# Three edits to a hybrid decoder layer in split FP32 on one core: the first two projection slots interleaved by k step, two weight units in other buffers, a fixed order for the last group

## Chip, core and metric

The kernel runs on one NeuronCore of one Trainium2 chip, in one launch. The metric is the device time of one execution in microseconds (us). Engines are named as in the profile: PE is TensorE, ACT is ScalarE, DVE is VectorE, POOL is GpSimd, SP is SyncE, which here only issues transfers.

## What is computed

One decoder layer on x of 512 tokens and 1024 channels, all in float32:

```python
u = rms_norm(x, norm_mix_pre)
proj = u @ w_in                    # ten slots of 256 columns, four gates of 1024
y_a, y_b, y_c, y_d = ...           # gated recurrence, pooling, HGRN2, short convolution
branch_out = einsum("btkc,kcd->btkd", ys, w_branch)
merged = sum_k sigmoid(gate_k) * branch_out_k
h = x + rms_norm(merged @ w_out, norm_mix_post)
u = rms_norm(h, norm_mlp_pre)
hid = square(relu(u @ w_up))       # 4096 wide
h = h + rms_norm(hid @ w_down, norm_mlp_post)
```

## The kernel before, in words

**Products in three passes.** Every large product is taken from operands that are split into a high and a low half. `split` (L160) lets ACT make the high half (a rounding copy) and DVE the low half (the difference). `mm3` (L240) then adds three matmuls: high by high, high by low, low by high. A matmul has 128 rows, 128 columns of weights and mostly 512 moving columns.

**Weights.** All weights but the down projection's come in units of 128x1024 (512 KB) from `wts`. `load` (L149) issues the transfers on SP into three raw buffers, `prep` (L164) splits a unit into one of six pairs `whi`, `wlo`, and `unit` (L232) hands out the next one while it prepares up to four units ahead. `Wt` holds the counters. Units 66 and 67, the last two of the output projection, are an exception (`SPARE`): they go into two tiles of the pool `up`. That pool has four tiles, which first hold `uh` and `ul`, the halves of the transposed input (L257), and later `u2h` and `u2l`, the halves of the second norm's output (L860).

**The start (L276 to L294, L358).** The input comes transposed in eight tiles of 128x512 (`xT`, `xload` L146), one for each k step of the contraction. `xsplit` (L265) scales a tile by `gmix`, a column of the parameter tile `par_s`, and makes its two halves. The first unit is cut in three (`LOADCUT`). Eight small matmuls on a tile of ones (`WARM`) run while the first transfers come. Then `slot_mm` (L336) makes one slot of 256 columns: for each of eight k steps two column halves of 128 with three matmuls each, into two PSUM banks. A slot needs two units, k steps 0 to 3 and 4 to 7. Slots follow one another: `b0`, `b1`, `b2`, then `p_x` and so on. The pool `mm` of PSUM has four banks, which `b0` and `b1` fill. `b2` lies in the pool `sm`. The fourth slot, `p_x` (L385), takes the four banks over once `evac` (L349) has multiplied the sums by `rstd_bc`. That is the token norm, which comes from `do_rstd` (L316) and is spread over the partitions by two matmuls in `bc_rstd` (L330), called in the middle of `b2`.

**The output projection (L782 to L894).** `e0` makes columns 0 to 511 of four token tiles. `out_mm` (L829) makes columns 512 to 1023 of one token tile, with units 64 to 67 in `wu`. `chain` (L843) turns the sums of a tile into h and into the input of the up projection: square and sum, root (`row_rstd`), two passes over 1024 columns. `trans` and `put` (L863, L872) transpose it and split it, `put(t, 0, ..)` for k steps 0 to 3 into `u2h[0]`, `u2l[0]`, `put(t, 1, ..)` for k steps 4 to 7 into `u2h[1]`, `u2l[1]`. The first up projection (`up_mm`, L906) starts with k steps 0 to 3 of tokens 0 to 255.

**The MLP.** `up_pair` (L968) makes 256 hidden columns, `up_out` (L919) takes relu (ACT), square (ACT) and the split. `down_group` multiplies groups of 512 hidden channels by a scheme of seven products. Only the last group (L1038 to L1070) is made plainly: four units `us`, two hidden pairs `aa[0]` and `aa[1]` (pairs 14 and 15), and for each token tile t two pieces of 512 columns, the last tile's second piece in two of 256. Each piece is added to `macc` (L1052), squared and summed (`sq_only`, `sq_tot`), multiplied by the gain (`gain`, L1029). After the root (`row_rstd`, L812) `half` (L1032) scales, adds h and sends the result out.

**What sets the order.** The kernel is written in Tile, which places the instructions of each engine by a simulated timeline, so the order of the program differs from that of the text, except for calls inside `keep_in_program_order`. On the chip each engine's queue runs strictly in the order placed, and waits on semaphores.

Of the kernel before, what the change touches and what calls it, by code (L numbers as in the profile page):

```python
# [41 lines left out]
for _n, _w in (("gmix", 8), ("convw", 8), ("convb", 2), ("ba", 2), ("bx", 2), ("lam", 2),  # L42
               ("pscale", 2), ("lb", 2), ("hnorm", 1), ("sconv", 6), ("invw", 2), ("corr", 32), ("bo", 2)):
    PAR[_n] = (_o, _w)
    _o += _w
# [4 lines left out]
def tile_hybrid_trunk(ctx: ExitStack, tc: tile.TileContext, xT, xn, wts, dn, par, bd, cst, msk, gains, out):  # L50
# [65 lines left out]

    xt = [ap_.tile([P, 2, T], F32, tag="acc", name=nm("xt")) for _ in range(4)]
# [24 lines left out]
    spare = []  # L142
    LOADCUT = {0: ((0, 256), (256, 512), (512, D))}
    xfirst = [0, 1, 2]

    def xload(k):  # L146
        nc.sync.dma_start(xt[k // 2][:, k % 2], xT[k])

    def load(n):  # L149
        while Wt.n_load < min(n, NU):  # L150
            i = Wt.n_load
            r = rp.tile([P, D], F32, tag="raw", name=nm("raw"))
            for o, e in LOADCUT.get(i, ((0, D),)):
                if i == 0 and xfirst:
                    xload(xfirst.pop(0))
                nc.sync.dma_start(r[:, o:e], wts[i, :, o:e])
            Wt.raw[i] = r
            Wt.n_load += 1
# [5 lines left out]
    def prep(n):  # L164
        while Wt.n_prep < min(n, NI):
# [15 lines left out]
            for o, e in LOADCUT.get(i, ((0, D),)):  # L181
                if i == 0 and xorder[0] == 0:
                    xorder.pop(0)
                    xsplit(0, lambda: split(hi[:, o:e], lo[:, o:e], r[:, o:e]))
                    continue
                split(hi[:, o:e], lo[:, o:e], r[:, o:e])
                if i == 0:
                    xsplit(xorder.pop(0))
# [39 lines left out]
    extra = []  # L228
    ahead = [4]
    WARM = 8  # L230

    def unit():  # L232
# [3 lines left out]
        if extra:  # L236
            extra.pop(0)()
# [25 lines left out]
    xorder = [0, 1, 2]  # L263

    def xsplit(k, between=None):  # L265
        src = xt[k // 2][:, k % 2]
        g = prm("gmix", k)
# [4 lines left out]
        if between:  # L272
            between()
# [4 lines left out]
    act.activation(wrm, ones[:, :1].bitcast(F32), AF.Sigmoid)  # L278
    nc.scalar.dma_start(par_s[:, :NPAR], par)
    load(1)  # L280
# [3 lines left out]
    xload(3)  # L284
    load(2)
    for k in range(4, NK):
        xload(k)
    load(3)
    prep(1)
    xsplit(3)  # L290
    prep(2)
    for k in range(4, NK):
        xsplit(k)
# [18 lines left out]
    extra[:] = [lambda: load_x(0), lambda: load_x(1), lambda: load_x(2), lambda: load_x(3), load_consts]  # L312
# [45 lines left out]
    b0 = slot_mm()  # L358
    b1 = slot_mm()
# [668 lines left out]

    def gain(t, a, b):  # L1029
        dve.tensor_tensor(mgs[t][:, a:b], cm(t, a, b), g2[:, a:b], ALU.mult)  # L1030

    def half(t, r, a, b):  # L1032
        m = mgs[t][:, a:b]
        dve.scalar_tensor_tensor(m, m, r, hr[t // 2][:, t % 2, a:b], ALU.mult, ALU.add)
        eng = nc.scalar if t == NT - 1 and a == T else nc.sync
        eng.dma_start(out[t * P : t * P + P, a:b], m)

    us = [unit() for _ in range(GF)]  # L1038
    aa = [[x_[:, :4].rearrange("p (c h) t -> p c (h t)", c=2) for x_ in hid.pop(NPAIR - 2 + s)] for s in range(2)]
    for t in range(NT):  # L1040
        bk = dn_bank()
        pieces = [(0, T, bk[:, 0]), (T, 2 * T, bk[:, 1])]
        if t == NT - 1:
            pieces[1:] = [(T, T + 256, bk[:, 1, :256]), (T + 256, D, up_bank()[:, 0, :256])]
        for pi, (a, b, ps) in enumerate(pieces):
# [5 lines left out]
            m = cm(t, a, b)  # L1051
            dve.tensor_tensor(m, m, ps, ALU.add)  # L1052
            sq_only(m, 4 + t, pi)
            if pi < 1 or t < NT - 1:
                v = sq_tot(4 + t, pi, stat[:, t, 6:7] if pi == 0 else v, 3 + pi)
            if pi == 0:
                mgs[t] = hp.tile([P, D], F32, tag="h", name=nm("mg"))
            if t < NT - 1 or pi < 2:
                gain(t, a, b)
        if t == NT - 1:  # L1060
            v = sq_tot(4 + t, 1, v, 4)
            v = sq_tot(4 + t, 2, v, 5)
        r = row_rstd(v, 4 + t, (lambda: gain(t, T + 256, D)) if t == NT - 1 else None)
        if t == NT - 1:
            half(t, r, 0, T)
            half(t, r, T, T + 256)
            half(t, r, T + 256, D)
        else:
            for a, b in ((0, T), (T, D)):
                half(t, r, a, b)  # L1070


def _layout(inp):
# [5 lines left out]
    xt = x.T.reshape(NK, P, T)  # L1079
    xn = x.reshape(NT, P, D)  # L1080
# [12 lines left out]
    for n in SLOT_ORDER:  # L1093
        slot(wi, SLOT[n])
    for k in GATE_ORDER:
# [23 lines left out]
    def cols(v):  # L1119
# [6 lines left out]
        a["norm_mix_pre"][0].reshape(8, P).T,  # L1126
# [26 lines left out]
    return [xt, xn, wts, dn, par, bd, cst, msk, gains]  # L1153
# [21 lines left out]
```

## Time and profile before

| | us |
|---|---|
| median of 3 runs (751.07 to 751.37) | 751.09 |
| profiled execution, its own time | 751.62 |
| its span, first to last instruction | 749.8 |
| PE busy in the span | 738.3 (98%) |
| DVE busy | 537.7 (72%) |
| ACT busy | 312.2 (42%) |

The span runs from the first to the last instruction on the core; the execution's own time is taken around it. PE's busy time includes matmuls that overlap in the pipeline: one of 512 columns takes 0.39 from its start to its end, and in a dense row the next one starts well before that end. So the starts of matmuls tell more than their busy time.

### The profile page before, as it was taken

How to read it: one execution, taken by the hardware profiler on the slowest of the kernel's cores; microseconds unless marked ns; L12 is line 12 of the kernel's file. 1: busy time of each engine (PE TensorE's matmuls, PEld its weight loads, DVE VectorE, ACT ScalarE, POOL GpSimd, SP SyncE). 2: the span in 40 equal slices, each digit the busy share in tenths (PEclk: the TensorE clock that was granted, in tenths of full speed). 3: DMA queues.
4: the chain of work that ended last, by engine and by line, in shares of the span. 5: the costliest groups of instructions: out<-in, count | busy, mean ns of one | idle time of the engine just before them, and what ended most of it. 6: DMA issues, size and time to landing. Idle time of an engine off the chain costs nothing.

```text
span 749.8 us, 8896 instructions
## 1 busy us (share of the span) xinstructions
PE 738.3 (98%) x3508; PEld 620.5 (83%) x3508; DVE 537.7 (72%) x781; ACT 312.2 (42%) x404; POOL 6.3 (1%) x11
## 2 busy tenths in 40 slices
PE   8999999999999999999999999999999999999995
PEld 7888988888888888888888988888888888888884
DVE  5798346559997576554649585787879696977967
ACT  6524223335423322242445466544445362636322
POOL 1100000000000000000000000000000000000000
PEclk9999999999999999999999999999999999999998
DMA  9733232222222253223333514142323314050202
GB/s 327 265 116 112 85 102 95 85 85 85 84 75 95 85 185 124 98 100 111 113 113 140 202 52 169 57 140 85 135 89 109 116 64 161 6 214 33 84 1 112
DMA packets 23049, 84.59 MB, mean 113 GB/s; under 512 B 2656, under 2 KB 3424, under 8 KB 21216
## 3 DMA queue, kind: packets, MB, share of 16 engines
q1 hardware_dynamic: 22720, 83.86, 31.6%
q8 instruction: 27, 0.44, 0.2%
q10 hardware_dynamic: 288, 0.17, 0.1%
q14 instruction: 14, 0.11, 0.0%
HBM read 79.83 MB, written 4.19 MB: 112 GB/s over the span
## 4 chain that ended last, share of the span: by engine, by line
PE 96%; DVE 2%; DMA 1%; issue 1%; SPq 0%; ACT 0%; DVEq 0%; ACTq 0%
PE mm L242 15%; PE mm L243 15%; PE mm L241 15%; PE ub L241 8%; PE ub L243 8%; PE ub L242 8%; PE db L243 7%; PE db L241 7%; PE db L242 7%; PE sm L571 2%; PE sm L243 1%; PE sm L242 1%; PE sm L241 1%; DMA raw<-in_wts_dram 1%; PE sm L680 0%
## 5 line engine op out<-in xcount | busy, mean ns | idle before, releaser
L161 ACT ACTIVATE whi<-raw 128x1024 fp32r<-128x1024 f32 (+2 forms) x104 | 108.7, 1045 | 250.0 <-PE mm L242 123.1
L162 DVE TENSOR_TENSOR wlo<-raw,whi 128x1024 fp32r<-128x1024 f32 (+2 forms) x104 | 124.8, 1200 | 74.0 <-ACT whi L161 73.4
L242 PE MATMUL mm<-ul,whi 128*128 128x512 f32 x384 | 149.7, 391 | 0.6 <-DVE ul L274 0.6
L243 PE MATMUL mm<-uh,wlo 128*128 128x512 f32 x384 | 149.2, 390 | 0.0
L241 PE MATMUL mm<-uh,whi 128*128 128x512 f32 x384 | 148.8, 393 | 0.4 <-ACT whi L161 0.4
L241 PE MATMUL ub<-u2h,whi 128*128 128x512 f32 (+1 forms) x288 | 105.4, 367 | 1.0 <-DVE u2l L162 1.0
L242 PE MATMUL ub<-u2l,whi 128*128 128x512 f32 (+1 forms) x288 | 105.3, 366 | 0.0
L243 PE MATMUL ub<-u2h,wlo 128*128 128x512 f32 (+1 forms) x288 | 105.2, 366 | 0.0
L242 PEld LDWEIGHTS mm<-ul,whi 128*128 128x128 f32 x384 | 72.3, 189 | 16.0 <-DVE ul L274 1.2
L241 PEld LDWEIGHTS mm<-uh,whi 128*128 128x128 f32 x384 | 72.1, 188 | 15.8 <-ACT whi L161 0.9
L243 PEld LDWEIGHTS mm<-uh,wlo 128*128 128x128 f32 x384 | 72.4, 188 | 15.0
L242 PE MATMUL db<-flo,ahi 128*128 128x512 f32 x196 | 76.3, 389 | 0.0
L241 PE MATMUL db<-fhi,ahi 128*128 128x512 f32 x196 | 76.3, 389 | 0.0
L243 PE MATMUL db<-fhi,alo 128*128 128x512 f32 x196 | 76.3, 389 | 0.0
L992 DVE TENSOR_TENSOR macc<-macc,db 128x1024 f32<-128x1024 f32 x42 | 51.1, 1216 | 23.1 <-PE db L243 22.4
L241 PEld LDWEIGHTS ub<-u2h,whi 128*128 128x128 f32 x288 | 54.2, 189 | 10.1 <-DVE u2l L162 1.4
L242 PEld LDWEIGHTS ub<-u2l,whi 128*128 128x128 f32 x288 | 54.3, 189 | 8.8
L243 PEld LDWEIGHTS ub<-u2h,wlo 128*128 128x128 f32 x288 | 54.3, 189 | 8.7
L161 ACT ACTIVATE fhi<-x 128x1024 fp32r<-128x1024 f32 x28 | 29.7, 1059 | 39.8 <-PE db L243 26.6
L242 PEld LDWEIGHTS db<-flo,ahi 128*128 128x128 f32 x196 | 36.8, 188 | 7.7
L241 PEld LDWEIGHTS db<-fhi,ahi 128*128 128x128 f32 x196 | 36.8, 188 | 7.6
L243 PEld LDWEIGHTS db<-fhi,alo 128*128 128x128 f32 x196 | 36.8, 188 | 7.6
(271 smaller groups left out, 1024.3 us busy)
## 6 DMA issues: line engine op xcount, KB each, us to landing
raw<-in_wts_dram SPq DMA_DIRECT2D x103, 512.0 KB, 3.3
ab<-in_dn_dram SPq DMA_DIRECT2D x14, 1024.0 KB, 4.8
t<-in_xn_dram SPq DMA_DIRECT2D x8, 512.0 KB, 8.0
xt<-in_xt_dram SPq DMA_DIRECT2D x8, 256.0 KB, 5.5
h1d<-t SPq DMA_DIRECT2D x4, 512.0 KB, 2.7
hr<-h1d SPq DMA_DIRECT2D x2, 1024.0 KB, 5.4
out_dram<-mg SPq DMA_DIRECT2D x7, 256.0 KB, 2.0
t<-in_gains_dram SPq DMA_DIRECT2D x2, 512.0 KB, 6.2
```

The source lines that it names most:

```text
L161: act.activation(hi, src, AF.Copy)
L162: dve.tensor_tensor(lo, src, hi.bitcast(F32), ALU.subtract)
L241: pe.matmul(ps, lh, rh, start=first, stop=False)
L242: pe.matmul(ps, lh, rl, start=False, stop=False)
L243: pe.matmul(ps, ll, rh, start=False, stop=last)
L571: pe.matmul(bk[ct][:, cs].rearrange("s (h n b) -> s h n b", h=2, b=B), kk_[:, ct, cs], qo, start=True, stop=True)
L992: dve.tensor_tensor(macc[p], macc[p], ps, ALU.add)
```

## The change

Three edits, with a smaller layout change for the first.

1. The first two slots run together. `x0` is a new input, the first x tile with the eight columns of `gmix` beside it, so `par_s` loses these. Units 1 and 2 are swapped in the layout, so that units 0 and 1 are k steps 0 to 3 of both slots and units 2 and 3 k steps 4 to 7. Each k step has twelve matmuls: both slots, both column halves, three passes. Units 0 and 1 come in three cuts, the very first piece on ACT's queue. The token tiles, two more units and the constants are loaded behind (`extra` is gone), and there are seven small matmuls instead of eight.
2. Units 66 and 67 are split into tiles of the pool `acc`, the buffers of the merged branches.
3. The last group's instructions are kept in program order on PE, DVE and ACT, with the finishing of tile t - 1 (`finish`) written behind the first piece of tile t. The last tile's scaling is done in parts of 768 and 256 columns instead of 512, 256 and 256.

The core of the diff:

```diff
-    LOADCUT = {0: ((0, 256), (256, 512), (512, D))}
...
+        if k == 0:
+            nc.sync.dma_start(x0t, x0)
+        else:
+            nc.sync.dma_start(xt[k // 2][:, k % 2], xT[k - 1])
...
             if i in SPARE:
-                if not spare:
-                    spare.extend(up.tile([P, 2, D], F32R, tag="u", name=nm("sp")) for _ in range(2))
-                hi, lo = (x_[:, i - SPARE[0]] for x_ in spare)
+                hi, lo = (ap_.tile([P, D], F32R, tag="acc", name=nm("sp")) for _ in range(2))
...
+    wload(nc.scalar, 0, 0, W)
     nc.scalar.dma_start(par_s[:, :NPAR], par)
+    xload(0)
+    wload(nc.sync, 1, 0, W)
+    xload(1)
+    wload(nc.sync, 0, W, 2 * W)
+    wload(nc.sync, 1, W, 2 * W)
+    xload(2)
...
+    CUTS = {0: (0, W), 1: (W, 2 * W), 2: (2 * W, D), 4: (0, 2 * W), 6: (2 * W, D)}
+    for k in range(NK):
+        pair = (0, 1) if k < 4 else (2, 3)
+        if k in CUTS:
+            o, e = CUTS[k]
+            act.activation(fw[pair[0]][0][:, o:e], fr[pair[0]][:, o:e], AF.Copy)
+        xhi(k)
+        if k in CUTS:
+            act.activation(fw[pair[1]][0][:, o:e], fr[pair[1]][:, o:e], AF.Copy)
+        xlo(k)
+        if k in CUTS:
+            for i in pair:
+                dve.tensor_tensor(fw[i][1][:, o:e], fr[i][:, o:e], fw[i][0][:, o:e].bitcast(F32), ALU.subtract)
+        for wi, us_, first, last in ((0, uh, True, False), (0, ul, False, False), (1, uh, False, True)):
+            for s_ in range(2):
+                for c in range(2):
+                    o_ = (k % 4) * W + c * P
+                    pe.matmul(fb[s_][c], fw[pair[s_]][wi][:, o_ : o_ + P], U(us_, k),
+                              start=first and k == 0, stop=last and k == NK - 1)
...
-    b0 = slot_mm()
-    b1 = slot_mm()
     dg = do_rstd()
...
+    def add_sq(t, pi, a, b, ps):
+        m = cm(t, a, b)
+        K(dve.tensor_tensor(m, m, ps, ALU.add))
+        K(act.activation(s_tile(b - a), m, AF.Square, accum_out=stat[:, 4 + t, pi : pi + 1]))
...
+    def finish(t, rhw, cut):
+        rt, h, w = rhw
+        r = stat[:, 4 + t, 7:8]
+        K(dve.reciprocal(r, rt))
+        K(dve.scalar_tensor_tensor(w, r, h, r, ALU.mult, ALU.mult))
+        K(dve.scalar_tensor_tensor(r, w, 1.5, r, ALU.add, ALU.mult))
+        half(t, r, 0, cut)
+        half(t, r, cut, D)
...
+        for a, b, ps in pieces:
             for j in range(GF):
                 wh, wl = us[j]
-                hh, hl = aa[j // 2]
-                mm3(ps, hh[:, j % 2, t * P : t * P + P], hl[:, j % 2, t * P : t * P + P],
-                    wh[:, a:b], wl[:, a:b], j == 0, j == GF - 1)
...
+                hh, hl = (x_[:, j % 2, t * P : t * P + P] for x_ in aa[j // 2])
+                K(pe.matmul(ps, hh, wh[:, a:b], start=j == 0, stop=False))
+                K(pe.matmul(ps, hh, wl[:, a:b], start=False, stop=False))
+                K(pe.matmul(ps, hl, wh[:, a:b], start=False, stop=j == GF - 1))
+        mgs[t] = hp.tile([P, D], F32, tag="h", name=nm("mg"))
+        for pi, (a, b, ps) in enumerate(pieces):
+            add_sq(t, pi, a, b, ps)
+            if pi == 0 and prev:
+                finish(t - 1, prev, T)
+            gain(t, a, b)
+            v = tot(t, pi)
+        prev = root(v)
+    finish(NT - 1, prev, T + 256)
```

Where the order of instructions moves, at three places. First PE in the second half of the third slot (`sm_344`, `sm_345`), up to the first matmul of the fourth, `p_x`. Before (`sm_390` is the sum of `bc_rstd`, `mm_443` the first half of `p_x`; 2 and 17 matmuls of the third slot are left out at the two gaps):

```order
L241 MATMUL sm_344<-uh_109,whi_247 128x512
L332 MATMUL sm_390<-t_335,ones 128x512
L242 MATMUL sm_344<-ul_111,whi_247 128x512
...
L242 MATMUL sm_345<-ul_111,whi_247 128x512
L333 MATMUL sm_390<-t_335,ones 128x512
L243 MATMUL sm_345<-uh_109,wlo_248 128x512
...
L243 MATMUL sm_345<-uh_109,wlo_248 128x512
L241 MATMUL mm_443<-uh_108,whi_279 128x512
```

and now (`sm_400` is that sum, `mm_453` the half of `p_x`, in the bank of `mm_153`; eight and five matmuls of the third slot are left out at the two gaps):

```order
L231 MATMUL sm_345<-uh_110,wlo_353 128x512
L359 MATMUL sm_400<-t_335,ones 128x512
L229 MATMUL sm_344<-uh_110,whi_352 128x512
...
L229 MATMUL sm_345<-uh_110,whi_352 128x512
L360 MATMUL sm_400<-t_335,ones 128x512
L230 MATMUL sm_345<-ul_112,whi_352 128x512
L231 MATMUL sm_345<-uh_110,wlo_353 128x512
...
L231 MATMUL sm_345<-uh_110,wlo_353 128x512
L229 MATMUL mm_453<-uh_109,whi_358 128x512
```

The second of the pair, L333 before and L360 now, stands 19 matmuls of the third slot ahead of `p_x` before, and eight now. The third slot's first matmul is on both sides the 97th after the small ones.

Second DVE in the chain of token tile 2 of the output projection, up to the low half that the first up projection waits for. Before (`u2l_3110` is `u2l[0]`, `u2l_3151` is `u2l[1]`):

```order
L162 TENSOR_TENSOR u2l_3110<-sm_3099,u2h_3109 128x4x128
L821 RECIPROCAL stat<-rt_3088 128x1
L822 SCALAR_TENSOR_TENSOR nt_3090<-stat,nh_3089 128x1
L823 SCALAR_TENSOR_TENSOR stat<-nt_3090,stat 128x1
L848 SCALAR_TENSOR_TENSOR t_2808<-t_2969,stat,t_2808 128x1024
L162 TENSOR_TENSOR wlo_3286<-raw_2956,whi_3285 128x1024
L850 SCALAR_TENSOR_TENSOR t_2969<-t_2808,rst_101,t_2801 128x1024
L162 TENSOR_TENSOR wlo_3506<-raw_3246,whi_3505 128x1024
L162 TENSOR_TENSOR u2l_3110<-mm_3126,u2h_3109 128x4x128
L162 TENSOR_TENSOR u2l_3151<-sm_3104,u2h_3150 128x4x128
```

and now (`u2l_3122` is `u2l[0]`, `u2l_3163` is `u2l[1]`):

```order
L162 TENSOR_TENSOR u2l_3122<-sm_3111,u2h_3121 128x4x128
L846 RECIPROCAL stat<-rt_3100 128x1
L162 TENSOR_TENSOR u2l_3163<-sm_3116,u2h_3162 128x4x128
L847 SCALAR_TENSOR_TENSOR nt_3102<-stat,nh_3101 128x1
L848 SCALAR_TENSOR_TENSOR stat<-nt_3102,stat 128x1
L873 SCALAR_TENSOR_TENSOR t_2818<-t_2981,stat,t_2818 128x1024
L162 TENSOR_TENSOR wlo_3298<-raw_2968,whi_3297 128x1024
L875 SCALAR_TENSOR_TENSOR t_2981<-t_2818,rst_101,t_2811 128x1024
L162 TENSOR_TENSOR wlo_3518<-raw_3258,whi_3517 128x1024
L162 TENSOR_TENSOR u2l_3122<-mm_3138,u2h_3121 128x4x128
L162 TENSOR_TENSOR u2l_3163<-mm_3143,u2h_3162 128x4x128
```

One low half of `u2l[1]` moves from behind the last row on `u2l[0]` to the place behind the reciprocal.

Third PE at the start of the last group, behind the last matmul of up pair 15. Before (`ahi_5313` and `alo_5314` are `aa[0]`, `ahi_5520` and `alo_5521` are `aa[1]`; `db_5534`, `ub_5679`, `db_5582` are three pieces):

```order
L241 MATMUL db_5534<-whi_5459,ahi_5313 128x512
L243 MATMUL db_5534<-whi_5459,alo_5314 128x512
L241 MATMUL ub_5679<-whi_5431,ahi_5313 128x256
L242 MATMUL ub_5679<-wlo_5432,ahi_5313 128x256
...
L242 MATMUL db_5582<-wlo_5460,ahi_5313 128x512
L243 MATMUL db_5582<-whi_5459,alo_5314 128x512
L243 MATMUL ub_5679<-whi_5459,alo_5314 128x256
L241 MATMUL db_5534<-whi_5489,ahi_5520 128x512
L242 MATMUL db_5534<-wlo_5490,ahi_5520 128x512
...
L243 MATMUL db_5534<-whi_5489,alo_5521 128x512
```

and now (`ahi_5325`, `alo_5326` are `aa[0]`; `ahi_5532`, `alo_5533` are `aa[1]`; `db_5546` is tile 0's bank):

```order
L231 MATMUL ub_5470<-u2h_3162,wlo_5424 128x512
L1103 MATMUL db_5546<-whi_5443,ahi_5325 128x512
L1104 MATMUL db_5546<-wlo_5444,ahi_5325 128x512
L1105 MATMUL db_5546<-whi_5443,alo_5326 128x512
...
L1105 MATMUL db_5546<-whi_5471,alo_5326 128x512
L1103 MATMUL db_5546<-whi_5501,ahi_5532 128x512
L1104 MATMUL db_5546<-wlo_5502,ahi_5532 128x512
L1105 MATMUL db_5546<-whi_5501,alo_5533 128x512
```

Before, 18 matmuls on `aa[0]` stand ahead of the first one on `aa[1]`, and six more ahead of the first one on its low half; now there are six, and two more.

## Rows read from the trace of the kernel before

**Rows 1.** The page, the chain of work that ended last, by engine.

```profile
PE 96%; DVE 2%; DMA 1%; issue 1%; SPq 0%; ACT 0%; DVEq 0%; ACTq 0%
```

**Rows 2.** Timeline, 0 to 9 us: start us, duration us, engine, line, operation, [idle before].

```profile
1.05 3.79 PE L283 MATMUL sm<-ones 128*128 128x128 f32 x16 [1.05 <-DVE spt L526]
...
3.79 0.49 DVE L269 TENSOR_SCALAR uh<-xt,par_s 128x512 fp32r<-128x512 f32 x1 [2.79 <-DMA par_s<-in_par_dram]
...
4.59 1.22 PE L241 MATMUL mm<-uh,whi 128*128 128x512 f32 x2
...
5.61 1.05 PE L242 MATMUL mm<-ul,whi 128*128 128x512 f32 x2
...
6.47 0.78 PE L243 MATMUL mm<-uh,wlo 128*128 128x512 f32 x2
6.58 0.72 ACT L271 ACTIVATE uh<-xt,par_s 128x512 fp32r<-128x512 f32 x1 [2.03 <-DMA xt<-in_xt_dram]
...
8.23 0.64 PE L242 MATMUL mm<-ul,whi 128*128 128x512 f32 x2
```

**Rows 3.** Two stretches: bounds, busy us of each engine, granted clock, DMA share, GB/s.

```profile
9.00:12.00 3.00, 3.00 (x15) 2.21 (x13) 1.98 (x4) 2.25 (x4) 0.00 (x0) 1.00 1.05 406
408.40:416.00 7.60, 7.58 (x64) 7.58 (x65) 6.94 (x34) 6.22 (x20) 0.00 (x0) 1.00 0.36 139
```

**Rows 4.** Timeline, third slot to the start of the fourth.

```profile
29.30 0.39 PE L241 MATMUL sm<-uh,whi 128*128 128x512 f32 x1
...
36.11 0.40 PE L333 MATMUL sm<-t,ones 128*128 128x512 f32 x1
...
36.54 0.69 DVE L334 COPY rstd_bc<-sm 128x512 f32<-128x512 f32 x1
...
37.35 1.23 DVE L162 TENSOR_TENSOR wlo<-raw,whi 128x1024 fp32r<-128x1024 f32 x1
...
38.49 2.48 DVE L350 TENSOR_TENSOR t<-mm,rstd_bc 128x512 f32<-128x512 f32 x4
...
40.65 0.39 PE L241 MATMUL mm<-uh,whi 128*128 128x512 f32 x1
```

**Rows 5.** Timeline, end of the output projection, start of the up projection.

```profile
402.38 0.15 DVE L821 RECIPROCAL stat<-rt 128x1 f32<-128x1 f32 x1
402.57 0.22 DVE L822 SCALAR_TENSOR_TENSOR nt<-stat,nh 128x1 f32<-128x1 f32 x1
...
407.07 0.39 PE L243 MATMUL sm<-sp,ylo 128*128 128x512 f32 x1
...
407.68 0.69 DVE L162 TENSOR_TENSOR u2l<-mm,u2h 128x512 fp32r<-128x512 f32 x1
...
408.42 0.39 PE L241 MATMUL ub<-u2h,whi 128*128 128x256 f32 x1 [0.96 <-DVE u2l L162]
```

**Rows 6.** Timeline, start of the last group.

```profile
718.91 0.39 PE L241 MATMUL db<-whi,ahi 128*128 128x512 f32 x1
...
719.11 1.03 ACT L921 ACTIVATE q<-ub 128x1024 f32<-128x1024 f32 x1 [7.32 <-PE ub L243]
...
722.35 1.23 DVE L162 TENSOR_TENSOR alo<-q,ahi 128x1024 fp32r<-128x1024 f32 x1 [3.37 <-ACT ahi L161]
...
722.37 0.50 PE L241 MATMUL db<-whi,ahi 128*128 128x512 f32 x1
...
723.64 0.49 PE L243 MATMUL db<-whi,alo 128*128 128x512 f32 x1
```

**Rows 7.** Timeline of the end; then DVE's groups from 720 to 747 us.

```profile
740.98 0.28 PE L243 MATMUL db<-whi,alo 128*128 128x256 f32 x1
...
745.16 1.54 DVE L1034 SCALAR_TENSOR_TENSOR mg<-mg,stat,hr 128x512 f32<-128x512 f32 x3
...
L1034 DVE SCALAR_TENSOR_TENSOR mg<-mg,stat,hr 128x512 f32<-128x512 f32 x7 | 5.0, 747 | 0.1
L1030 DVE TENSOR_TENSOR mg<-macc,g 128x512 f32<-128x512 f32 x7 | 4.8, 688 | 0.1
```

More of the change, by code (lines that the diff above doesn't have):

```diff
@@ L49, in tile_hybrid_trunk @@
 @with_exitstack
-def tile_hybrid_trunk(ctx: ExitStack, tc: tile.TileContext, xT, xn, wts, dn, par, bd, cst, msk, gains, out):
+def tile_hybrid_trunk(ctx: ExitStack, tc: tile.TileContext, x0, xT, xn, wts, dn, par, bd, cst, msk, gains, out):
     nc = tc.nc
@@ L115, in prm @@
         return par_s[:, o + i : o + i + w]
+    x0t = cx_.tile([P, T + NK], F32, name="x0t")
     xt = [ap_.tile([P, 2, T], F32, tag="acc", name=nm("xt")) for _ in range(4)]
@@ L152, in load @@
             r = rp.tile([P, D], F32, tag="raw", name=nm("raw"))
[L153 to L156, printed above, removed]
+            if i >= NFIRST:
+                nc.sync.dma_start(r, wts[i])
             Wt.raw[i] = r
@@ L180, in prep @@
                 lo = wp.tile([P, D], F32R, tag="wlo", name=nm("wlo"))
[L181 to L188, printed above, removed]
+            split(hi, lo, r)
             Wt.hl[item] = (hi, lo)
@@ L261, in U, with xhi @@
         return lst[k // 4][:, k % 4, a:b]
[L263 to L267, printed above, removed]
+    def xhi(k):
+        src = x0t[:, :T] if k == 0 else xt[k // 2][:, k % 2]
+        g = x0t[:, T + k : T + k + 1]
         if k == 0:
@@ L283, in tile_hybrid_trunk @@
         pe.matmul(wb[:, :P], ones.bitcast(F32), ones.bitcast(F32), start=True, stop=True)
-    xload(3)
-    load(2)
-    for k in range(4, NK):
-        xload(k)
[L288 to L293, printed above, removed]
+    xload(4)
+    load(3)
+    wload(nc.sync, 2, 0, D)
+    load(4)
+    wload(nc.sync, 3, 0, D)
+    for k in range(5, NK):
+        xload(k)
+    fw = [(wp.tile([P, D], F32R, tag="whi", name=nm("whi")), wp.tile([P, D], F32R, tag="wlo", name=nm("wlo")))
+          for _ in range(NFIRST)]
+    fr = [Wt.raw.pop(i) for i in range(NFIRST)]
+    fb = [[mm_bank(), mm_bank()] for _ in range(2)]
+    CUTS = {0: (0, W), 1: (W, 2 * W), 2: (2 * W, D), 4: (0, 2 * W), 6: (2 * W, D)}
[17 more added lines that the diff above has]
+                              start=first and k == 0, stop=last and k == NK - 1)
+    b0, b1 = fb
+    Wt.n_prep = use[0] = NFIRST
     xns = []
@@ L310, in load_consts @@
         pool.memset(sbd, 0.0)
-    extra[:] = [lambda: load_x(0), lambda: load_x(1), lambda: load_x(2), lambda: load_x(3), load_consts]
+    for t in range(NT):
+        load_x(t)
+    load(6)
+    load_consts()
     ssq = cx_.tile([P, NT], F32, name="ssq")
@@ new lines, in root @@
+    def root(v):
+        rt, h, w = (npool.tile([P, 32], F32, tag=g, name=nm(g))[:, :1] for g in ("ni", "nh", "nt"))
+        K(act.activation(rt, v, AF.Sqrt))
+        K(dve.tensor_scalar(h, v, -0.5, None, ALU.mult))
+        return rt, h, w
+    def finish(t, rhw, cut):
[6 more added lines that the diff above has]
+        half(t, r, cut, D)
@@ L1094, in _layout @@
         slot(wi, SLOT[n])
+    units[1], units[2] = units[2], units[1]
     for k in GATE_ORDER:
```

66 lines of the change are left out of this document (27 added, 39 removed).

## The prediction

> **What bounds the kernel now.** I read the chain of waits first: 96% of the span is TensorE [rows 1]. So only four kinds of place can move the time: where TensorE waits, where it runs slowly, how the last results leave after its last matmul, and where a new order makes it wait anew. I then went through its matmul starts for gaps. The reader is to see three. At the start the first matmul of the first slot begins at 4.59 us, the next ones come 0.43 us apart (two in 5.61 to 6.47), and only the two from 8.23 on stand at the later pace (0.64 for both, where 5.61 took 1.05); ACT meanwhile waits 2.03 us for the second x tile, until 6.58 [rows 2]. In the middle there is one hole, 407.07 to 408.42, released by a `u2l` half on DVE [rows 5]. After the last matmul's start at 740.98 the span goes on to 749.8. Elsewhere matmuls of 512 columns follow each other at 0.227 us: 50 of them from 29.30 to 40.65 [rows 4].
>
> The profiled execution took 751.62 us (span 749.8), 0.53 more than the median 751.09. I add up against the profiled one and carry the difference over to the median. A measurement of this kernel can tell about 0.2%, 1.5 us, from no change.
>
> **First two slots, k by k: 1.95 us less.** Both slots together are 96 matmuls, 21.8 us at 0.227. They now take from 4.59 to 29.30, 24.7 us, so 2.9 are lost [rows 2, 4]. About 1.1 of that is the slow pace: five or six matmuls at 0.43 instead of 0.227 until the pace changes near 6.8. The other 1.8 is supply: one x tile and one 256-column piece of weights feed only six matmuls, 1.36 us. In the new order an x tile with two pieces (512 KB in all) feeds twelve, 2.73 us, while 512 KB take 1.3 us at the 406 GB/s of the stretch from 9 to 12 us [rows 3]. The second x tile, in SP's queue behind one more piece of 128 KB (0.3 us at that rate), would land at 6.8 instead of about 6.5; its twelve matmuls are due at about 8.3. So no step after the first waits. The first matmul: DVE waited for the parameters until 3.79 [rows 2], which now ride with the x tile; one warm-up matmul of eight goes, 0.45 us of the 3.79; but two pieces have to be there. I take 4.45. Then 4.45 + 1.1 + 21.8 gives 27.35 for the start of the third slot, against 29.30. Bounds: no loss but the pace and a start at 4.2 give 2.2 less; a first step that waits another 0.9 for its second piece gives 1.0 less.
> The first piece of weights now goes through ACT's queue. The parameters went there before, and though they are only 35 KB they were waited for as long as the 256 KB tile on SP. The Trainium skill, DMA: Bandwidth & Descriptors, section "Issuing engines are not separate DMA queues", says that both queues feed the same 16 engines and only issue time is saved; by that the second queue brings nothing here beyond one issue, and the trace agrees.
>
> **A wait at the fourth slot: 0.9 us more.** The four PSUM banks of the first two slots are needed again by the fourth slot, `p_x`, and come free when DVE scales them by `rstd_bc`. That waits for the matmul pair of `bc_rstd`. The second of the pair starts at 36.11; DVE's copy starts at 36.54, one weight half follows, then the first scaling, 38.49 and 0.69 long [rows 4]: about 3.05 from the matmul's start until the first bank is free. Before, 20 starts lay between (36.11 to 40.65, 4.5 us), a margin of 1.5. In the new order only nine do, 2.05 us. So TensorE waits 1.0, less the 0.1 by which the weight half itself waited for ACT here. Bounds: nothing if DVE were through 1 us sooner; 1.3 if a weight half before the copy is late. That the other waits of these slots stay covered rests on the preparation, which runs four units, 96 matmuls or 22 us, ahead.
>
> **Units 66 and 67 in the merged branches' buffers: 0.5 us more.** They no longer block half of the `u` buffers, so `put(0, 1)` can run before the last output matmul. But DVE is full there. The scheduler now puts that `u2l` half (0.69 long, 0.6 when packed) between the reciprocal and the next step of tile 2's root, ahead of the half that TensorE waits for at 408.42 [rows 5]. About 0.1 of it fills the pause after the reciprocal (402.38 to 402.57). What got earlier, nobody waited for. So the hole of 1.1 us grows by 0.5. Unit 67's own preparation goes behind the last merged tile, some 7 us later; its first matmul is more than 10 us after that, and the raw buffer that it frees late serves units of the next phase: nothing. Bounds: -0.2 if the pause hides more, 0.6.
>
> **Last group in program order: 2.8 us more.** This is the largest term. The last group needs the activations of the last two pairs, `aa[0]` and `aa[1]`. TensorE starts the group at 718.91, when the last up projection has just ended; then ACT makes relu, square and the high half from 719.11 on, and DVE the low half (722.35, 1.23 long). The old order fills this time: it runs what needs `aa[0]` alone of three different pieces, comes to the first matmul on the new high half at 722.37 and on the new low half at 723.64 [rows 6]. Between 718.91 and 723.64 it starts 16 matmuls of 512 columns and 8 of 256, 4.55 us of work in 4.73, so it loses only 0.15. The new order has six matmuls on `aa[0]`, 1.36 us, and then asks for `aa[1]`. It waits from 720.27 to 722.37 (2.1), runs two (0.45), and waits for the low half until 723.63 (0.8). With about 0.1 for each resumption, less the 0.15, the last matmul starts 2.8 later. All the matmuls thus skipped still have to run. Bounds: 2.3 and 3.0; DVE, ACT and the order ahead of the group are unchanged, so I see no way for it to be small.
>
> **The tail: 0.4 us less.** Count from the last matmul's start. Before, the last scaling (three parts, 1.54) began 4.18 after it, at 745.16 [rows 7]. Now tile 3's first piece is added from about 2.5 before that point on (24 half-width matmuls, 2.9 us, less one matmul's own 0.4). Behind it stand in DVE's fixed order: that add, three small steps of tile 2's root, its two scalings, a gain, then twice an add and a gain of 256 columns with ACT's square and its sum behind each, and the root. By the rows of 512 columns (0.69, scalings 0.75, a tenth less each when packed) [rows 7] and a bit over half of that for 256, I estimate 0.6 + 0.65 + 1.35 + 0.6, twice 1.05, and 1.05: 6.35, so the last scaling begins 3.85 after the last matmul: 0.33 earlier, and as two parts it is 0.1 shorter. The single transfer of 384 KB behind it lands no sooner than the small ones did. I take 0.4. Bounds: 0, and 2.0 if DVE had no backlog and only tile 3's own last piece stood behind the last matmul (rival A).
>
> **Sum.** -1.95 + 0.9 + 0.5 + 2.8 - 0.4 = +1.85. The profiled execution would take 753.5, the median 752.95, say 753.0: 0.25% slower.
>
> **Rivals.**
> A. The tail gains most. Fixed orders let tile 2 be finished ahead of tile 3's second piece; if DVE is through with tile 2 when that piece comes, the last scaling starts some 2.2 after the last matmul instead of 4.2. The sum is then +0.2: 751.3, no slower. For it: today tiles 2 and 3 are finished together, the scalings one behind the other up to 746.70 [rows 7]. Against it: the sum of DVE's rows above. It decides if that scaling starts less than 2.6 after the last matmul.
> B. No wait at `p_x` and the full start: -2.2, 0, +0.5, +2.8, -0.4 = +0.7: 751.8. It needs DVE's copy and scaling within 2.05 of the matmul. The old rows show 3.05.
> C. TensorE's pace falls in the last group. It has two levels, 1.2 and 2.4 GHz, and the first rows show the lower one. If 2.1 and 0.8 us of idling with two matmuls between bring it back and it lasts as long as at the start (matmuls from 1.05 on, fast near 6.8, 5.7 us), half of that is lost: +2.9 more, 755.9. Against it: after the hole at 408 the granted clock is 1.00, the upper level [rows 3].
> The Trainium skill, TensorE: Matmul & The Clock Gate, section "HAM oscillation — how this bites in real kernels", describes just this, idle waits after which matmuls start cold; no run here shows whether this wait is enough.
> D. The start gains nothing: the pieces of both slots compete with the second x tile so that TensorE idles in the first two steps as long as before. Then +3.8: 754.9. Against it: the 2.73 us of work per x tile.
>
> **How the numbers follow.** My own case 0.58, A 0.17, B 0.13, C 0.06, D 0.06. My case has its five terms each uncertain by some tenths, so about 0.10 of its 0.58 lies under +1.5. Slower by over 0.2%: 0.48 + 0.06 + 0.06 = 0.60. Faster by over 0.2% would need A and B together with a smaller wait in the last group: 0.03. The rest, 0.37, is within. The range goes from A with the larger start (750.7) to D (754.9) and leaves C out.
>
> **What would show it.** In the new profile: first matmul of slot three near 27.4; TensorE waiting about 0.9 for a DVE scaling at the first `mm` matmul of `p_x`; a hole of 1.6 before the first `ub` matmul; six matmuls in the last group, then waits of 2.1 for ACT's `ahi` and 0.8 for DVE's `alo`; the last scaling 3.9 after the last matmul. Wrong it is if the last group shows no such waits, or if the tail is shorter by more than 1 us.

## The result, and the profile after

The changed kernel takes 757.58 us in the median of four runs (757.14 to 759.84), the kernel before 751.23 beside it: a ratio of 1.009 (95% interval 1.007 to 1.0111), 6.35 us slower. The forecast was 753.0 with a range from 750.7 to 754.9. The sign was right; the size lies outside.

The profiled execution took 759.84 (span 758.0), 2.3 above its own median. Where that comes from is seen below. The chain by engine, which answers to [rows 1], has 4% of DMA where there was 1%, and TensorE's share falls from 96% to 91%:

```profile
PE 91%; DMA 4%; DVE 3%; ACT 1%; issue 1%; SPq 0%; DVEq 0%; ACTq 0%
```

The timeline from the first matmul to the fourth slot (start, duration, engine, line, operation, idle time before), the answer to [rows 2, 4]:

```profile
4.55 1.26 PE L314 MATMUL mm<-uh,whi 128*128 128x512 f32 x4
...
26.50 0.39 PE L229 MATMUL sm<-uh,whi 128*128 128x512 f32 x1
...
35.80 0.40 PE L360 MATMUL sm<-t,ones 128*128 128x512 f32 x1
...
36.26 1.22 DVE L162 TENSOR_TENSOR wlo<-raw,whi 128x1024 fp32r<-128x1024 f32 x1 [1.35 <-ACT whi L161]
37.40 0.68 DVE L361 COPY rstd_bc<-sm 128x512 f32<-128x512 f32 x1
...
37.62 0.39 PE L231 MATMUL sm<-uh,wlo 128*128 128x512 f32 x1
...
38.95 1.23 DVE L162 TENSOR_TENSOR wlo<-raw,whi 128x1024 fp32r<-128x1024 f32 x1 [0.87 <-ACT whi L161]
40.10 2.48 DVE L377 TENSOR_TENSOR t<-mm,rstd_bc 128x512 f32<-128x512 f32 x4
...
40.93 0.47 PE L229 MATMUL mm<-uh,whi 128*128 128x512 f32 x1 [2.92 <-ACT whi L161]
...
42.49 0.63 PE L229 MATMUL mm<-uh,whi 128*128 128x512 f32 x1
42.92 0.63 PE L230 MATMUL mm<-ul,whi 128*128 128x512 f32 x1
```

The third slot starts at 26.50 instead of 29.30: 2.80 gained, more than the 1.95 forecast. Then the fourth slot starts at 40.93, later than the 40.65 of before: all of it is given back in a wait of 2.9 on TensorE, 3.31 from start to start (37.62 to 40.93). And some of the matmuls behind it come 0.43 us apart. The view names ACT's high half as what ended the wait, and the chain follows that half back through the transfers ahead of it; most of its 4% of DMA comes from there. Whether that half was waited for is tested below.

The end of the output projection and the last group, the answer to [rows 5 to 7]:

```profile
409.03 0.39 PE L231 MATMUL sm<-sp,ylo 128*128 128x512 f32 x1
410.85 0.39 PE L229 MATMUL ub<-u2h,whi 128*128 128x256 f32 x1 [1.43 <-DVE u2l L162]
...
721.33 0.39 PE L1103 MATMUL db<-whi,ahi 128*128 128x512 f32 x1
...
722.46 0.39 PE L1105 MATMUL db<-whi,alo 128*128 128x512 f32 x1
724.78 0.70 PE L1103 MATMUL db<-whi,ahi 128*128 128x512 f32 x1 [1.94 <-ACT ahi L161]
...
726.04 0.80 PE L1105 MATMUL db<-whi,alo 128*128 128x512 f32 x1
726.64 0.63 PE L1103 MATMUL db<-whi,ahi 128*128 128x512 f32 x1
...
730.63 0.39 PE L1105 MATMUL db<-whi,alo 128*128 128x512 f32 x1
...
731.06 0.69 DVE L1067 TENSOR_TENSOR macc<-macc,db 128x512 f32<-128x512 f32 x1 [5.07 <-PE db L1105]
...
746.99 0.68 DVE L1067 TENSOR_TENSOR macc<-macc,db 128x512 f32<-128x512 f32 x1
...
747.21 0.28 PE L1105 MATMUL ub<-whi,alo 128*128 128x256 f32 x1
...
753.47 1.41 DVE L1061 SCALAR_TENSOR_TENSOR mg<-mg,stat,hr 128x768 f32<-128x768 f32 x2
```

The hole in the middle is 1.82 from start to start where it was 1.35. The last group, from its first to its last matmul, takes 25.88 (721.33 to 747.21) where it took 22.07. And the last scaling begins 6.26 after the last matmul, where 4.18 was measured before and 3.85 forecast. TensorE's clock by stretches (bounds, busy us of PE, PEld, DVE, ACT, POOL, granted clock, DMA share, GB/s):

```profile
42.10:46.00 3.90, 3.90 (x11) 3.06 (x11) 3.90 (x6) 0.00 (x0) 0.00 (x0) 0.56 0.40 119
724.80:728.40 3.60, 3.46 (x8) 2.27 (x9) 1.19 (x1) 0.00 (x0) 0.00 (x0) 0.53 0.00 0
728.40:732.00 3.60, 3.60 (x18) 2.96 (x17) 0.91 (x2) 0.22 (x1) 0.00 (x0) 1.00 0.00 0
```

Behind both waits the mean granted clock is 0.56 and 0.53 of full speed, near the lower of its two levels (1.2 and 2.4 GHz). The whole difference of this execution, span against span, 8.2:

| part | forecast | measured in the profiled execution |
|---|---|---|
| start, to the third slot | -1.95 | -2.80 |
| wait at the fourth slot | +0.9 | +3.08 |
| slow pace behind it | not forecast | +1.68 |
| hole in the middle | +0.5 | +0.47 |
| last group, first to last matmul | +2.8 | +3.81 |
| tail, last matmul's start to the end of the span | -0.4 | +2.0 |

No other profiled kernel below that has the first edit shows the slow pace behind the fourth slot, so the 1.68 probably belong to this execution, which is the slowest of its four; the other three were not traced.

### The profile page after: what moved, and what is told of

The parts are those of the page before. It is cut to its first block, busy times and chain, and to the rows that moved or that the text cites. A ratio compares the mean times of both kernels' runs of the same rounds, so it can differ in the third digit from the quotient of the medians.

```text
span 758.0 us, 8901 instructions
## 1 busy us (share of the span) xinstructions
PE 739.9 (98%) x3506; PEld 621.4 (82%) x3506; DVE 537.6 (71%) x784; ACT 313.5 (41%) x408; POOL 7.2 (1%) x11
## 4 chain that ended last, share of the span: by engine, by line
PE 91%; DMA 4%; DVE 3%; ACT 1%; issue 1%; SPq 0%; DVEq 0%; ACTq 0%
PE mm L229 14%; PE mm L231 14%; PE mm L230 14%; PE ub L229 8%; PE ub L230 8%; PE ub L231 8%; PE db L231 6%; PE db L230 6%; PE db L229 6%; DMA raw<-in_wts_dram 4%; PE sm L596 2%; PE sm L231 1%; PE sm L229 1%; PE sm L230 1%; PE db L1105 1%
## 5 line engine op out<-in xcount | busy, mean ns | idle before, releaser
L161 ACT ACTIVATE whi<-raw 128x1024 fp32r<-128x1024 f32 x98 | 104.0, 1061 | 251.4 <-PE mm L230 119.2
L162 DVE TENSOR_TENSOR wlo<-raw,whi 128x1024 fp32r<-128x1024 f32 x98 | 119.6, 1220 | 78.7 <-ACT whi L161 78.5
L229 PE MATMUL mm<-uh,whi 128*128 128x512 f32 x352 | 137.6, 393 | 2.9 <-ACT whi L161 2.9
L231 PE MATMUL mm<-uh,wlo 128*128 128x512 f32 x352 | 137.8, 392 | 0.0
L230 PE MATMUL mm<-ul,whi 128*128 128x512 f32 x352 | 137.7, 391 | 0.0
L229 PEld LDWEIGHTS mm<-uh,whi 128*128 128x128 f32 x352 | 66.4, 189 | 16.8 <-ACT whi L161 3.3
L231 PEld LDWEIGHTS mm<-uh,wlo 128*128 128x128 f32 x352 | 66.5, 189 | 13.9
L230 PEld LDWEIGHTS mm<-ul,whi 128*128 128x128 f32 x352 | 66.5, 189 | 13.8
```

What stands on the lines that cost most here:

```text
L161: act.activation(hi, src, AF.Copy)
L162: dve.tensor_tensor(lo, src, hi.bitcast(F32), ALU.subtract)
L229: pe.matmul(ps, lh, rh, start=first, stop=False)
L230: pe.matmul(ps, lh, rl, start=False, stop=False)
L231: pe.matmul(ps, ll, rh, start=False, stop=last)
```

## The experiments

Three theories were formed from this trace. Theory 1: the fixed order costs twice, in the last group and behind it. Theory 2: the wait at the fourth slot is DVE's. Theory 3: the tail is a matter of what an add waits for. The kernel before, run beside them, takes 751.23 on the chip of the first four (third edit undone, third edit alone, free bank, adds between) and 751.10 on that of the next four (DVE's order, separate banks, and both of the last group). Differences to the changed kernel (757.58) are uncertain by that 0.13.

### The parts by themselves

The third edit undone (the last group's text as before):

> The last group and the tail are written as before the change; the first two edits stay. Theory 1 (the fixed order costs twice, in the last group, +3.8 us from its first to its last matmul, and behind it, +2.0): the group takes 22.1 us and the span ends 8.8 us after the last matmul's start, as before, so 5.8 less than the changed kernel: 751.8 to 753.6, the upper end if the profiled execution's terms of the start (-2.8 +3.1 +1.7) and the middle (+0.5) hold in every run. Rival (most of the loss sits in the start, and the last group only shows it): 756 or more.

751.27 (ratio 1.0, 0.9991 to 1.0009), a little under the lower end of theory 1. The first two edits together are worth nothing: the third slot starts at 26.96, and the fourth at 40.28 after a wait of 1.81. The rows of the fourth slot:

```profile
39.45 1.88 DVE L377 TENSOR_TENSOR t<-mm,rstd_bc 128x512 f32<-128x512 f32 x3
...
40.28 0.47 PE L229 MATMUL mm<-uh,whi 128*128 128x512 f32 x1 [1.81 <-DVE t L377]
```

The third edit alone, on the kernel before:

> The kernel before with the third edit alone. Theory 1: +5.8 on 751.2, 757.0; first wait of the last group 2.1 us, then 0.3 and 0.5, then some seven matmuls 0.43 us apart; last scaling 6.3 us after the last matmul. Rival of the prediction (2.8 for the waits, -0.4 for the tail, no slow pace): 753.6.

756.51 (1.0071, 1.0056 to 1.0086): 5.3 of the 6.35 are the third edit's. Group 24.85, last scaling 6.26 after the last matmul. The profiled execution has the two waits, but not the seven slow matmuls that theory 1 expected; its matmuls behind the second wait come 0.23 apart at once:

```profile
721.79 0.50 PE L1078 MATMUL db<-whi,ahi 128*128 128x512 f32 x1 [1.94 <-ACT ahi L161]
...
723.05 0.50 PE L1080 MATMUL db<-whi,alo 128*128 128x512 f32 x1 [0.53 <-DVE alo L162]
723.38 0.40 PE L1078 MATMUL db<-whi,ahi 128*128 128x512 f32 x1
723.62 0.40 PE L1079 MATMUL db<-wlo,ahi 128*128 128x512 f32 x1
```

24.85 less the 22.07 of before is 2.78: the waits alone, as the prediction priced them.

### The fourth slot

First a bank that is free, instead of an earlier release:

```diff
-    bs = slot_mm()
+    bs = slot_mm_c(sm_bank())
```

`slot_mm_c` runs all k steps of the first column half into that bank, then those of the second half into a bank of `mm`.

> The changed kernel, but the fourth slot takes its first half column into a PSUM bank that is free (the one of the warm-up matmuls) and only its second half, 24 matmuls or 5.4 us later, into a bank of the first two slots. Theory 2 (TensorE waits for DVE's scaling of the bank, which is late because DVE stands behind weight halves that wait for their transfers; the idling brings the slow pace): no wait there, no matmuls 0.43 us apart behind it, 4.8 us less: 752.8. Rival (the weights of the fourth slot are late, as the releaser named by the view of waits says, ACT's high half): the wait stays about 3 us, 757.6.

756.93: only 0.65 less, but the wait is gone: 11.35 us from the third slot to the fourth (27.49 to 38.84), the 50 dense matmuls of [rows 4]. So it was not the weights, though the view of waits named ACT's high half there: that half, which ends at 40.90, is one of a later unit. Theory 2 holds on the wait; its 4.8 was far too much. The slow pace that it counted was in no other trace, and part of the gain is lost in the middle, presumably because the banks rotate differently from then on. The first `ub` matmul there waits for the second of two `u2l` halves, and the hole grows from 1.82 to 2.42:

```profile
406.29 1.28 DVE L162 TENSOR_TENSOR u2l<-mm,u2h 128x512 fp32r<-128x512 f32 x2
...
407.62 0.38 PE L229 MATMUL ub<-u2h,whi 128*128 128x256 f32 x1 [2.03 <-DVE u2l L162]
```

Then the other side, DVE's order alone:

```diff
-            split(hi, lo, r)
+            if i in (9, 10):
+                act.activation(hi, r, AF.Copy)
+                KE(dve.tensor_tensor(lo, r, hi.bitcast(F32), ALU.subtract))
+            else:
+                split(hi, lo, r)
...
-        dve.tensor_copy(rstd_bc, ps)
+        KE(dve.tensor_copy(rstd_bc, ps))
```

`KE` is `keep_in_program_order`; the four scalings of the first two slots have it too.

> The changed kernel with one change in DVE's order: the copy of the token norm and the four scalings that free the banks of the first two slots stand ahead of the low halves of units 9 and 10, which stood before and between them. Theory 2 (the wait at the fourth slot is for these scalings, and they stand behind weight halves that wait for their transfers): the copy starts near 36.5 us, the first scaling ends near 37.2, TensorE comes to the fourth slot without a wait; 1 to 3 us less, as the start was slow or fast: 755.6. Rival (the wait only moves: the units 9 and 10 are then late for the fifth slot): 757 or more, with a wait of TensorE for a low half between 45 and 55 us.

755.84 (1.0061, 1.0044 to 1.0078), 1.74 less than the changed kernel; theory 2 to 0.2 us, and no wait behind it for the two units. The rows:

```profile
36.59 0.69 DVE L366 COPY rstd_bc<-sm 128x512 f32<-128x512 f32 x1 [2.83 <-PE sm L365]
37.31 2.48 DVE L382 TENSOR_TENSOR t<-mm,rstd_bc 128x512 f32<-128x512 f32 x4
...
38.20 0.42 PE L234 MATMUL mm<-uh,whi 128*128 128x512 f32 x1
```

Now DVE waits, 2.83 for the matmul pair, and not TensorE. The fourth slot starts at 38.20, 2.45 ahead of before.

### The tail

Each add written right behind its piece's matmuls:

```diff
-        for a, b, ps in pieces:
+        mgs[t] = hp.tile([P, D], F32, tag="h", name=nm("mg"))
+        for pi, (a, b, ps) in enumerate(pieces):
             for j in range(GF):
...
-        mgs[t] = hp.tile([P, D], F32, tag="h", name=nm("mg"))
-        for pi, (a, b, ps) in enumerate(pieces):
             add_sq(t, pi, a, b, ps)
```

> The changed kernel, with each piece's add written right behind that piece's matmuls instead of behind the matmuls of both pieces; the order on TensorE and DVE is the same instruction by instruction, only what the adds wait for differs. Theory 3 (the first add of a tile waits for the last matmul of the tile, 12 matmuls or 2.7 us too long, and DVE falls behind): last scaling begins 3.9 us after the last matmul's start instead of 6.3, 755.2. Rival (DVE's fixed order itself is too long for the end): 757.4 or more, last scaling still over 5.5 after.

760.04 (1.0113, 1.0098 to 1.0128): a miss, 2.5 slower than the changed kernel. Yet the tail got shorter, as theory 3 says, and by more: 7.46 instead of 10.82, the last scaling 2.9 after the last matmul where 3.9 was expected. TensorE pays for it:

```profile
733.80 0.39 PE L1106 MATMUL db<-whi,alo 128*128 128x512 f32 x1
734.97 0.50 PE L1104 MATMUL db<-whi,ahi 128*128 128x512 f32 x1 [0.78 <-DVE macc L1067]
```

The matmul at 734.97 is the first of a tile's second piece. It writes the other bank of the same tile `db`, and waits until DVE has read the first: 1.17 from start to start, where 0.23 is the dense step. This happens in each of the four tiles, and gives DVE time to catch up. The kernel before has its adds there too, but in its order pieces of different tiles alternate.

So each piece gets a PSUM tile of its own:

```diff
+    def piece_list(t):
+        r = [(0, T, dn_bank()[:, 0]), (T, D, up_bank()[:, 0])]
...
-        bk = dn_bank()
-        pieces = [(0, T, bk[:, 0]), (T, D, bk[:, 1])]
```

> The changed kernel with each add written right behind its piece, and each piece in a PSUM tile of its own (first pieces in the pool of the down projection, second pieces in that of the up projection). Theory 3 (waits go by whole tiles: an add waits for all matmuls into its tile that are written ahead of it, a matmul for all reads of its tile): the waits of 1.2 us at each tile that showed with the adds between are gone, the tail keeps its 7.5 us instead of 10.8, so 3.3 less than the changed kernel: 754.3. Rival (the waits belong to the banks, not to the tiles): 1.2 us at each tile as with the adds between, 760.

755.05 (1.0049, 1.0034 to 1.0064): 2.5 less than the changed kernel, where 3.3 was expected. The waits at each tile are gone; the tail is 8.50, not the 7.5 that it had with them:

```profile
742.56 0.69 DVE L1067 TENSOR_TENSOR macc<-macc,db 128x512 f32<-128x512 f32 x1 [0.31 <-PE db L1100]
...
745.11 0.28 PE L1100 MATMUL db<-whi,alo 128*128 128x256 f32 x1
...
749.05 1.42 DVE L1061 SCALAR_TENSOR_TENSOR mg<-mg,stat,hr 128x768 f32<-128x768 f32 x2
```

The last scaling begins 3.94 after the last matmul: the 3.85 that the prediction had worked out from DVE's rows. Theory 3 is shown by the pair: in this program, whole tiles are what is waited for, by the adds and by the matmuls.

### The last group

TensorE first on the first hidden pair, four pieces of it:

```diff
+    for t in range(2):
+        for a, b, ps in first[t]:
+            mms(t, a, b, ps, (0, 1))
```

> As with separate banks, and TensorE first runs what needs the first hidden pair alone, of the first two tiles, 24 matmuls or 5.4 us. Theory 1 (the last group loses 2.8 us to waits for the second pair's halves, and some 1.3 to the slow pace that the waits bring): no wait and no matmul 0.43 us apart in the last group, 4.1 less than with separate banks: 750.2. Rival (the slow pace comes anyway, as at other places of the run): only 2.8 less, 751.5.

751.99 (1.0012, 1.0003 to 1.0021). The group takes 21.79, 4.6 less, with no wait and no slow matmul; but only 3.1 of it arrive, so that the time alone lies nearer the rival's 751.5; the trace, without a slow matmul, speaks for theory 1 in the group. The tail grows to 9.61, because DVE sets the end. From its first add to the end of its last scaling it takes 21.26 (21.85 in the kernel before), and it is busy for 5.60 of the 6 us from 729 to 735. So a late first add counts, and it comes 7.0 us after the group's first matmul, where it was 5.95. The add before, then the rows of this kernel:

```profile
724.86 0.69 DVE L1052 TENSOR_TENSOR macc<-macc,db 128x512 f32<-128x512 f32 x1 [1.28 <-PE db L243]
```

```profile
725.44 0.69 DVE L1067 TENSOR_TENSOR macc<-macc,db 128x512 f32<-128x512 f32 x1 [2.33 <-PE db L1100]
...
745.29 1.41 DVE L1061 SCALAR_TENSOR_TENSOR mg<-mg,stat,hr 128x768 f32<-128x768 f32 x2
```

Then the waits with TensorE kept busy. The added matmuls go into a bank that nothing reads:

```diff
+                if t == 0 and a == 0 and j == 2:
+                    for _ in range(9):
+                        K(pe.matmul(bd_[:, 0], aa[0][0][:, 0, :P], us[0][0][:, :T], start=True, stop=True))
```

and three more of them ahead of the first matmul on the new low half.

> The changed kernel with TensorE kept busy in the two waits of the last group: nine matmuls of 512 columns ahead of the first one on the new high half, three ahead of the first one on the new low half, into a bank that nothing reads. The waits for the two halves stay. Theory 1 (idling brings the slow pace): no matmul 0.43 us apart behind the waits, 1 to 1.5 less than the changed kernel: 756.3. Rival (the pace falls for another reason, such as the new operands): same rows 0.43 us apart, 757.6 or more.

756.28 (1.007, 1.0055 to 1.0085), 1.3 less than the changed kernel, as theory 1 says. Timeline, then the stretches:

```profile
719.73 2.20 PE L1105 MATMUL ub<-whi,ahi 128*128 128x512 f32 x9
721.84 0.50 PE L1107 MATMUL db<-whi,ahi 128*128 128x512 f32 x1
722.18 0.40 PE L1108 MATMUL db<-wlo,ahi 128*128 128x512 f32 x1
722.42 0.86 PE L1111 MATMUL ub<-whi,ahi 128*128 128x512 f32 x3
723.12 0.47 PE L1112 MATMUL db<-whi,alo 128*128 128x512 f32 x1
723.43 0.40 PE L1107 MATMUL db<-whi,ahi 128*128 128x512 f32 x1
```

```profile
721.00:724.60 3.60, 3.60 (x17) 2.55 (x16) 1.23 (x1) 0.78 (x1) 0.00 (x0) 1.00 0.00 0
724.60:728.00 3.40, 3.40 (x17) 2.81 (x16) 0.92 (x2) 0.24 (x1) 0.00 (x0) 1.00 0.00 0
```

From its first real matmul (718.37) to its last (743.20) the group takes 24.83, the same as with the waits alone. So idling brings the slow pace, where it comes. This is one traced execution, and the third edit alone shows the waits without the pace; but the pace is in five of the six profiled kernels that idle there, and in none of the eight that do not. It costs 1.0 to 1.6: the groups of the changed kernel and of the kernels with a free bank, with DVE's order and with separate banks take 25.88, 26.48, 26.46 and 26.42.

### Versions that beat both

Four kernels on another chip, with 751.33 for the kernel before. Theories 4 and 5 of their expectations came from the runs above. The first edit with DVE's order mended, the other two undone:

> The first edit alone (second and third undone), with the scalings that free the first banks put ahead of the low halves of units 9 and 10. Theory 2: the fourth slot starts near 38.2 us instead of 40.65, and all behind it is as before the change, so 2.4 less than before: 748.7. Rival (what the start gains is given back at a later wait, for weights or in the middle): 750.5 or more.

748.81 (0.9971, 0.996 to 0.9981), 2.5 faster than before. The hole is 1.36, and the fourth slot starts 2.22 ahead of before:

```profile
38.43 0.42 PE L237 MATMUL mm<-uh,whi 128*128 128x512 f32 x1
```

The same with the second edit:

> As fixA, with the second edit kept. Theory 4 (the second edit costs what the low half on DVE takes that it lets run too early, 0.5): hole in the middle 1.82 instead of 1.35, 0.5 more than fixA, 749.2. Rival (the second edit changes nothing that can be measured): as fixA.

749.34 (0.9974, 0.9964 to 0.9985). The hole is 1.82, 0.46 longer, as theory 4 says of the trace; the two times are not told apart, since the intervals of their ratios overlap.

With a mended fixed order for the last group:

> As fixA, with the last group in a fixed order that avoids what the experiments showed: pieces in PSUM tiles of their own, each add behind its piece, TensorE first on what needs the first hidden pair alone of three pieces (18 matmuls), then all high halves of the first piece ahead of its low ones. Theory 5 (DVE sets the end: some 21.3 us from the first add to the last scaling's end, so the first add's start counts): first add 5.8 us after the group's start, end 0.7 earlier than fixA, 748.0. Rival (a fixed order is no better than the scheduler's even so): 748.7 or more.

748.52 (0.9966, 0.9954 to 0.9979), the fastest median, not told apart from the first. The first add comes 5.64 after the group's start (717.36), but the end of the span is only 0.2 nearer to that start than there, where 0.7 was expected: the last scaling does end 0.64 nearer, but the span ends 3.15 behind it, and 2.73 there. Against the kernel that starts with four pieces of the first pair, whose group is as long (21.79), the first add comes 1.36 earlier and the end 1.1: theory 5.

```profile
723.00 0.69 DVE L1075 TENSOR_TENSOR macc<-macc,db 128x512 f32<-128x512 f32 x1 [0.97 <-PE db L1110]
...
743.10 1.41 DVE L1069 SCALAR_TENSOR_TENSOR mg<-mg,stat,hr 128x768 f32<-128x768 f32 x2
```

And with the hole closed:

> As fixB, with the low halves of the units 70 and 71, 1.1 us each on DVE, put behind the low half that TensorE waits for in the middle. Theory 4 (the hole is DVE's queue): the hole of 1.35 us closes, 1.1 less than fixB: 746.9. Rival (the two units are then late for the next matmuls): a wait of about the same length some 5 us later, as fixB.

749.09 (0.9964, 0.9951 to 0.9978), as the one above: the rival. The hole is gone (405.40 to 405.63), and 11.5 us later TensorE waits for one of the two halves that were put back. Of the 1.2 gained against the kernel above, 1.0 is lost again there, and the rest by the start of the last group (717.52 against 717.36):

```profile
405.63 0.28 PE L238 MATMUL ub<-u2h,whi 128*128 128x256 f32 x1
...
417.09 0.39 PE L240 MATMUL ub<-u2h,wlo 128*128 128x256 f32 x1 [0.69 <-DVE wlo L186]
```

## Why the prediction was wrong in size, step by step

**The tail failed, by 2.4.** The step is the one that says that tile 3's first piece is added from about 2.5 before the last matmul's start, that is, when its own twelve matmuls are done. It is added 0.22 before (746.99 against 747.21); what stands behind that add took 6.48 to the last scaling, where the prediction had 6.35. In the new text both pieces' matmuls stand ahead of the first add, and the pieces are halves of one tile; the first add then waits for all 24 (731.06, just behind the matmul at 730.63). Tiles 0 to 2 get their first add 2.7 later for it, so DVE still has tile 2 to finish when the last matmul starts, and tile 3 piles up behind. With separate tiles and adds that wait for their own piece, tile 3's first add came 2.55 before the last matmul (742.56) and the last scaling 3.94 after it, within 0.1 of the forecast. No line of the diff adds a wait: it came from the place of the add in the text. The trace of the changed kernel has a sign of it on DVE: the first add of tile 0 waits for a semaphore of TensorE, the second for none.

**The wait at the fourth slot was mis-sized: 0.9 forecast, 0.95 to 3.08 measured** in six profiled kernels, the changed kernel's being the largest. The step took the 3.05 from the second matmul of the pair to the free bank from the old trace. In the changed kernel it is 4.98 (35.80 to 40.78), in the five others 2.86 to 3.88; the four of these whose third slot starts at 27.15 or later have 2.86 to 3.07 and a wait of 0.95 to 1.17, as forecast. So the mechanism was right, and the step held where the third slot starts about when it was forecast to (27.35). DVE's queue runs in order, and in the changed kernel the low half ahead of the copy and the one between copy and scaling both stood idle for transfers that landed at 35.06 and 37.76, 1.35 and 0.87 of idling. The prediction named such a half as its upper bound, 1.3, but counted only one. That preparation runs four units ahead was true of TensorE's needs, and beside the point: DVE waited for units that nobody needed yet. Since DVE sets when the slot starts, a faster start only makes the wait longer: the fourth slot came at 39.57 to 40.93 in all six profiled kernels that kept this order, whether the third began at 26.50 or at 27.63.

**The last group: the waits were right, the pace was added.** 2.8 forecast, 2.78 measured without the slow pace (24.85 against 22.07). Its waits and resumptions as written add up to 2.95; the count of skipped work, 4.55 less the 1.82 of eight matmuls, plus 0.1, gives the 2.8. The forecast gave the pace (rival C) 0.06 of chance and 2.9; it showed in most kernels with these waits, at 1.0 to 1.6. What spoke against it, a clock of 1.00 behind the hole of 0.96 us in the middle, was a shorter wait than these. And what it called the lower level at the start it had from the pace alone: the granted clock of that stretch of the kernel before, last but two in this row, reads 1.00 while matmuls come 0.43 apart.

```profile
4.50:6.00 1.50, 1.50 (x5) 1.20 (x5) 0.90 (x2) 0.04 (x1) 0.00 (x0) 1.00 0.92 259
```

The Trainium skill, TensorE: Matmul & The Clock Gate, section "HAM oscillation — how this bites in real kernels", says that idle waits leave the next matmuls cold. The trace agrees: 0.53 granted behind the waits, 1.00 with twelve matmuls in them. But it does not follow every time (1.00 behind the same waits in the third edit alone), and the waits of the page's example are longer than these.

**The start was right in the main.** Forecast -1.95, bounds -1.0 and -2.2; in the twelve profiled kernels with the first edit the third slot starts 1.65 to 2.80 earlier, in four of them beyond the bound. The forecast took 1.1 for the slow pace of the first matmuls as given; the fewer of them run at it, the earlier the third slot starts. The old start varies too: 28.73 with the third edit alone, against 29.30. **The middle was right**: 0.5 forecast, 0.47 measured, and the hole is 1.36 again with the second edit undone.

**The rivals.** A, a shorter tail, went the other way. B, no wait at the fourth slot, and D, no gain at the start, fell. The range left C out because of its small chance, and its lower end should be 751.1 and not 750.7 (A with the larger start adds up to 0.0); the lower end does not bear on the result. With the slow pace as measured the forecast would have been 754.0 to 754.6, with the tail as well 756.4 to 757.0.

The median's 6.35, put together anew from the other runs: start and fourth slot together -0.4 to -1.1, middle +0.5, waits +2.8, pace +1.0 to +1.6, tail +2.0 to +2.4: 5.2 to 6.9.

What stays open: why the two units' transfers land when they do. The traces show a part: each is issued when DVE's low half of the unit three before has been made and its raw buffer is free (30.92 behind a half that ends at 30.89, 33.11 behind 33.08), 1.8 and 1.3 later than in the kernel before. Units 5 and 6 had landed 2.7 and 2.3 later than before (26.14 and 27.39). The constant `bd` is now ahead of these two in SP's queue, and was behind unit 8; that this delays them was not tried.

## What to carry to other kernels

An instruction waits by the tile and by what the text has put ahead of it, so when code is moved, look at what each reader now waits for, not only at its place in the queue. A start that is made faster pays only up to the next resource that does not move with it; here it was an in-order queue that waited for data nobody needed yet, and putting the release ahead of it gave 2.5 us. An order that a scheduler found, with pieces of different tiles taking turns, can be doing three jobs at once: cover for a wait, for a shared tile, and for the engine behind.

## What was not expected of the hardware

The slow pace behind a wait does not come every time. The waits in the last group (1.94, and 0.53 behind it in all but the changed kernel, where the slow pace had begun) were followed by four to ten matmuls 0.43 us apart in five profiled kernels (granted clock 0.53 in the changed one), and by none in one with the same two waits, the third edit alone. At the fourth slot it came behind the wait of 2.92, and not behind those of 0.8 to 1.8 in five others. At the start, between none and five of the first steps were 0.40 us or longer in kernels with the same first instructions, and the third slot began between 26.50 and 27.65.
